# First modulation vector of a streaming-encoder layer: half of its weight rows go to TensorE, half stay on VectorE, and four token norms move behind the last VectorE sum

## The chip, the cores and the metric

The kernel runs on one core of one Trainium2 chip. A core has a matmul engine (TensorE, PE in the profile, with its weight loads shown as PEld), a vector engine (VectorE, DVE), an activation engine (ScalarE, ACT), a general engine (GpSimd, POOL) and a queue from which DMA transfers are issued (SyncE, SP). Each engine works through its own list of instructions in order and waits where an operand isn't there yet. The metric is the device time of one execution in microseconds (us); the median over runs is compared.

## The reference: what is computed

One layer of a transformer trunk over 1024 tokens of 1024 channels: a gated feed-forward block, a mixer with two kinds of attention, and a second feed-forward block. Ahead of each of the three, the tokens are normalised and modulated by a shift and a scale that come from one condition vector `c`:

```python
mod = (jax.nn.silu(c) @ w_ada[l] + b_ada[l]).reshape(b, N_SUB, 3, D_MODEL)
...
shift = mod[:, i, 0, None, :]
scale = mod[:, i, 1, None, :]
gate = mod[:, i, 2, None, :]
u = rms_norm(h, norm_pre[l, i]) * (1.0 + scale) + shift
return h + resid_w * gate * rms_norm(fn(u), norm_post[l, i])
```

The change touches the shift and scale of the first feed-forward block only (`i = 0`): a vector of 1024 values times a matrix of 1024 x 2048, in float32. Nothing of the first block's matmuls can use a channel before its shift and scale are known.

## The kernel before, in words

The matmuls of the feed-forward blocks work on float32 operands split into a high and a low part (`H` and `L`, type fp32r), three matmuls for each product. A 2x2 block scheme with seven products (Strassen's) is used for the three feed-forward matrices, so tokens come in two halves, channels in two halves.

The opening of the program is `start0_`. It loads the first 512 tokens (`xt[0..3]`, four tiles of 128 x 1024), normalises them on ScalarE, and then goes through four column blocks `cb` = 0 to 3. Block `cb` owns 256 channels of the shift and the same 256 of the scale, 512 columns in all. For each block:

- `matvec(cb)` loads the block's 1024 rows x 512 columns in four transfers of 512 KB (`w`, ring `row` of 8 buffers), two groups of 128 rows in each. Row group `k` is multiplied by the partition's own value of silu(c), `csil[:, k]`, and added up in `m` (128 x 512) on VectorE: one multiplication (L658) and seven multiply-adds (L660).
- TensorE sums `m` over its 128 partitions with a column of ones: four matmuls (L675) that write `mps`, 128 x 1 each. A float32 matmul shows as two instructions in the profile, so the profile counts 8 of L675 for a block. "The block's matvec products" below are these instructions.
- VectorE adds the bias and forms `bcol` and `acol`, the shift and scale as columns (L679 to L681).
- For the block's two channel groups `k`, TensorE transposes the four token tiles (L186), ScalarE applies scale and shift (`u`, L177), VectorE and GpSimd split it into `uH` (L179) and `uL` (L180).
- Feed-forward matmuls that need only the channels so far follow (L297 to L299, from `m.part`). Their weights come as `raw` tiles that ScalarE rounds to `wsH` and VectorE subtracts to `wsL` (L224, L225).

The sums of block `cb + 1` (`matvec(cb + 1)`) stand in the code ahead of block `cb`'s products. Tokens 512 to 1023 (`xt[4..7]`) are loaded during blocks 1 and 2 and normalised by `pre_norm` at the end of blocks 2 and 3: ScalarE squares and takes the root, VectorE inverts (L156) and scales the tile (L171). They are first used by the subtraction of the two token halves (L246) and by the transposes of `half1_blocks`, which feed the operands `T1`, `T2` and so on.

The order in which instructions stand on each engine is set by a scheduler that goes by its own estimates; `tc.keep_in_program_order` and `tc.issue_after` pin single instructions. SP issues a transfer only when the one eight places ahead of it has landed and the tile it fills is free.

Of the kernel before, what the change touches and what calls it, by code (L numbers as in the profile page):

```python
# [16 lines left out]
ALU = mybir.AluOpType  # L17
# [3 lines left out]
P = 128  # L21
D = 1024
S = 1024
NK = D // P
# [22 lines left out]
def build(ctx, tc, A, out):  # L47
    nc = tc.nc
    V, ACT, PE, POOL, SP = nc.vector, nc.scalar, nc.tensor, nc.gpsimd, nc.sync
# [10 lines left out]
    ones = const.tile([P, P], F32, name="ones")  # L60
# [4 lines left out]
    csil = const.tile([P, NK], F32, name="csil")  # L65
# [78 lines left out]
    def rstd_of(src, parts=1):  # L144

        junk = mpool.tile([P, D], BF16, name="junk", tag="junk", bufs=1)
        ss = mpool.tile([P, 2], F32, name="ss", tag="ss", bufs=4)
        w = D // parts
        for n in range(parts):
            ACT.activation(junk[:, n * w:(n + 1) * w], src[:, n * w:(n + 1) * w], AF.Square, scale=1.0 / 32.0, accum_out=ss[:, n:n + 1])  # L150
        if parts == 2:
            V.tensor_add(ss[:, 0:1], ss[:, 0:1], ss[:, 1:2])
        sq = mpool.tile([P, 1], F32, name="sq", tag="sq", bufs=4)
        ACT.activation(sq, ss[:, 0:1], AF.Sqrt, bias=eps)
        r = mpool.tile([P, 1], F32, name="rs", tag="rs", bufs=4)
        V.reciprocal(r, sq)  # L156
        return r
# [7 lines left out]
    def pre_norm(src, eng=V):  # L165

        r = rstd_of(src)
        if eng is ACT:
            ACT.mul(src, src, r)
        else:  # L170
            eng.tensor_scalar_mul(src, src, r)  # L171

    def modulate(mp, ps, k, half, ab, mtag="u32", bufs=3, eng=V):

        a, b = ab
        u32 = mp.tile([P, HALF], F32, name="u32", tag=mtag, bufs=bufs)
        ACT.activation(u32, ps, AF.Identity, bias=b[:, k:k + 1], scale=a[:, k:k + 1])  # L177
        H, L = u_tile("H", k, half), u_tile("L", k, half)
        V.tensor_copy(H, u32)  # L179
        eng.tensor_sub(L, u32, H.bitcast(F32))  # L180
        U[k, half] = (H, L)

    def transposed(psum, hn, k, half, tag):
        ps = psum.tile([P, HALF], F32, name="tps", tag=tag, **bank_bufs(tag))
        for q in range(4):
            PE.transpose(ps[:, q * P:(q + 1) * P], hn[4 * half + q][:, k * P:(k + 1) * P], ident)  # L186
        return ps
# [438 lines left out]
    xt = []  # L626

    def load_x(t):
        xt.append(y_tile(t))
        SP.dma_start(xt[t], A["x"][t * P:(t + 1) * P, :])  # L630

    def start0(fp, psum, mats):

        with tc.tile_pool(name="ff0", bufs=1, side="left", reuse_waits="tile") as sp:
            start0_(sp, fp, psum, mats)

    def start0_(sp, fp, psum, mats):
        raws = [sp.tile([P, 2, HALF], F32, name="raw0", tag="raw0", bufs=4) for _ in range(4)]
        for t in range(4):
            load_x(t)  # L640
        SP.dma_start(badaT, A["badaT"])
        SP.dma_start(npreT, A["npreT"])
        for t in range(4):
            pre_norm(xt[t], ACT)
        acol = const.tile([P, NK], F32, name="acol0")
        bcol = const.tile([P, NK], F32, name="bcol0")
        ab[0] = acol, bcol

        def matvec(cb):

            m = sp.tile([P, HALF], F32, name="m0", tag="m0", bufs=3)
            for kq in range(4):
                w = sp.tile([P, 2, HALF], F32, name="w0", tag="row", bufs=8)
                SP.dma_start(w, A["wada0"][cb, kq])
                for i in range(2):
                    cs = csil[:, 2 * kq + i:2 * kq + i + 1]
                    if kq == 0 and i == 0:
                        V.tensor_scalar_mul(m, w[:, i], cs)  # L658
                    else:
                        V.scalar_tensor_tensor(m, w[:, i], cs, m, ALU.mult, ALU.add)  # L660
            return m

        ms = [matvec(0)]
        for cb in range(4):
            ks = slice(2 * cb, 2 * cb + 2)
            if cb < 2:
                for i in (2 * cb, 2 * cb + 1):
                    mats[i].load(raws[i])
            for t in ((), (4, 5), (6, 7), ())[cb]:
                load_x(t)  # L670
            if cb < 3:
                ms.append(matvec(cb + 1))
            ps = psum.tile([P, HALF], F32, name="mps0", tag="y")
            for i in range(4):
                p = PE.matmul(ps[:, i:i + 1], ms[cb][:, i * P:(i + 1) * P], ones[:, 0:1], start=True, stop=True)  # L675
                if i == 0 and cb:

                    tc.keep_in_program_order(p)
            V.tensor_add(bcol[:, ks], ps[:, 0:2], badaT[:, ks])  # L679
            V.tensor_add(acol[:, ks], ps[:, 2:4], badaT[:, NK + 2 * cb:NK + 2 * cb + 2])  # L680
            V.scalar_tensor_tensor(acol[:, ks], acol[:, ks], 1.0, npreT[:, ks], ALU.add, ALU.mult)  # L681
            for k in (2 * cb, 2 * cb + 1):
                modulate(sp, transposed(psum, xt, k, 0, "y" if k % 2 == 0 else "pa"), k, 0, ab[0], mtag="u32", eng=V if cb == 3 else POOL)
            for t in ((), (), (4, 5), (6, 7))[cb]:
                pre_norm(xt[t])
            if cb < 2:
                for m in mats[:2]:
                    m.part()
            if cb == 1:
                for m in mats[2:4]:  # L690
                    m.part(2)
            if cb == 2:
                mats[0].part()
# [606 lines left out]
```

## Time and profile before

| | us |
|---|---|
| median of 3 runs | 2326.1 |
| lowest and highest run | 2325.53, 2331.6 |
| the profiled execution, its own time | 2332.79 |
| span of its trace, first to last instruction | 2331.0 |
| TensorE busy in the span | 2204.7 |
| VectorE busy in the span | 1570.6 |
| ScalarE busy in the span | 1047.5 |

Times in the trace count from the span's start. A busy TensorE isn't a TensorE at its peak: matmuls overlap each other, and the clock that is granted to the engine can be half of the full one. A row of the timeline gives start, duration, engine, line, operation, the tile written and the tiles read, how many instructions were merged, and in brackets how long the engine had been idle and what ended that.

### The profile page before, as it was taken

The page shows a single profiled execution, that of the slowest core. Times are in us where ns is not written, and L with a number is a line of the kernel's source. Part 1 is how long each engine was busy: PE and PEld are TensorE (multiplying, and loading weights), DVE is VectorE, ACT ScalarE, POOL GpSimd, SP SyncE. Part 2 cuts the span into 40 slices and gives each one's busy share as a digit, 9 for nine tenths or more (in the row PEclk, how much of TensorE's full clock was granted, in tenths as well). Part 3 has the DMA queues.
Part 4 walks back from the last instruction along what each step waited for, and adds up shares of the span by engine and source line. Part 5 has one row for each costly group of instructions (what it writes and reads, how often), then busy time and mean ns, then how long its engine had stood idle before and what let it go on. Part 6 is the DMA issues. An engine that isn't in the chain of part 4 may idle for free.

```text
span 2331.0 us, 28613 instructions
## 1 busy us (share of the span) xinstructions
PE 2204.7 (95%) x10420; PEld 1805.3 (77%) x10420; DVE 1570.6 (67%) x2612; ACT 1047.5 (45%) x1882; POOL 70.0 (3%) x90
## 2 busy tenths in 40 slices
PE   5989999989989989999999999999979999999998
PEld 3767788868868877878888888788767787877876
DVE  6885787566667587576677677665976666655565
ACT  4523333335445465454554455555723332325454
POOL 1000000000000010011001000000000000000000
PEclk8899999999999999999999999999989999999999
DMA  7283574358877211110111122764465443427667
GB/s 298 75 286 131 202 259 175 137 181 304 299 234 237 69 45 40 41 47 29 60 55 64 46 86 87 244 199 128 140 244 179 143 169 138 173 96 261 201 203 246
DMA packets 137678, 364.39 MB, mean 156 GB/s; under 512 B 16704, under 2 KB 20800, under 8 KB 137536
## 3 DMA queue, kind: packets, MB, share of 16 engines
q1 hardware_dynamic: 135904, 356.79, 45.0%
q0 software_dynamic: 1632, 5.77, 0.6%
q8 instruction: 81, 1.33, 0.2%
q14 instruction: 61, 0.50, 0.1%
HBM read 272.32 MB, written 90.18 MB: 156 GB/s over the span
## 4 chain that ended last, share of the span: by engine, by line
PE 67%; DVE 17%; DMA 8%; ACT 4%; issue 3%; SPq 0%; DVEq 0%; ACTq 0%
PE bank L299 9%; PE bank L297 9%; PE bank L298 9%; PE pps L765 4%; PE pps L763 4%; PE pps L767 4%; DMA stg<-in_wd 3%; DVE f L960 2%; PE bankA L547 2%; PE bankA L549 2%; PE bankA L548 2%; DMA stg<-d_T 2%; PE bankB L547 2%; PE bankB L548 2%; PE bankB L549 2%
## 5 line engine op out<-in xcount | busy, mean ns | idle before, releaser
L763 PE MATMUL pps<-uH,wsH 128*128 128x512 f32 x512 | 209.7, 410 | 0.0
L765 PE MATMUL pps<-uL,wsH 128*128 128x512 f32 x512 | 205.4, 401 | 0.0
L767 PE MATMUL pps<-uH,wsL 128*128 128x512 f32 x512 | 204.7, 400 | 0.0
L225 DVE TENSOR_TENSOR tbL<-stg,tbH 128x512 fp32r<-128x512 f32 x154 | 105.8, 689 | 113.7 <-ACT tbH L224 113.4
L224 ACT CAST tbH<-stg 128x512 fp32r<-128x512 f32 x154 | 95.6, 621 | 167.8 <-DMA stg<-d_T 98.6
L547 PE MATMUL bankA<-tbH,sbH 128*128 128x512 f32 x352 | 140.8, 402 | 18.3 <-ACT tbH L224 17.9
L297 PE MATMUL bank<-uH,wsH 128*128 128x512 f32 x352 | 141.4, 404 | 3.5 <-DVE uH L179 2.7
L298 PE MATMUL bank<-uL,wsH 128*128 128x512 f32 x352 | 140.3, 398 | 1.5 <-POOL uL L180 1.5
L548 PE MATMUL bankA<-tbL,sbH 128*128 128x512 f32 x352 | 140.4, 399 | 0.0
L549 PE MATMUL bankA<-tbH,sbL 128*128 128x512 f32 x352 | 139.6, 397 | 0.0
L299 PE MATMUL bank<-uH,wsL 128*128 128x512 f32 x352 | 139.2, 396 | 0.0
L224 ACT CAST wsH<-s 128x1024 fp32r<-128x1024 f32 x88 | 91.6, 1049 | 97.1 <-DVE s L331 88.0
L141 DVE TENSOR_TENSOR wsL<-raw,wsH 128x1024 fp32r<-128x1024 f32 x72 | 87.9, 1221 | 69.1 <-ACT wsH L140 67.5
L225 DVE TENSOR_TENSOR sbL<-stg,sbH 128x512 fp32r<-128x512 f32 (+1 forms) x176 | 108.8, 620 | 36.3 <-ACT sbH L224 34.6
L224 ACT CAST sbH<-stg 128x512 fp32r<-128x512 f32 (+1 forms) x176 | 98.9, 565 | 70.8 <-DMA stg<-hd_A 40.7
L364 ACT COPY q<-bank 128x512 f32<-128x512 f32 x44 | 25.8, 587 | 209.2 <-PE bank L299 209.2
L547 PE MATMUL bankB<-tbH,sbH 128*128 128x512 f32 x264 | 104.5, 396 | 11.3 <-ACT y L599 10.9
L767 PEld LDWEIGHTS pps<-uH,wsL 128*128 128x128 f32 x512 | 96.9, 189 | 17.9
L763 PEld LDWEIGHTS pps<-uH,wsH 128*128 128x128 f32 x512 | 97.6, 191 | 14.7
L225 DVE TENSOR_TENSOR wsL<-s,wsH 128x1024 fp32r<-128x1024 f32 x88 | 106.9, 1218 | 2.6 <-ACT wsH L224 2.0
L765 PEld LDWEIGHTS pps<-uL,wsH 128*128 128x128 f32 x512 | 97.2, 190 | 14.7
L548 PE MATMUL bankB<-tbL,sbH 128*128 128x512 f32 x264 | 104.2, 395 | 0.0
(247 smaller groups left out, 5947.7 us busy)
## 6 DMA issues: line engine op xcount, KB each, us to landing
wada<-in_wada SPq DMA_DIRECT2D x56, 512.0 KB, 5.6
raw<-in_wg SPq DMA_DIRECT2D x50, 512.0 KB, 6.7
raw<-in_wu SPq DMA_DIRECT2D x50, 512.0 KB, 4.4
raw<-in_wd SPq DMA_DIRECT2D x44, 512.0 KB, 4.5
stg<-hd_A SPq DMA_DIRECT2D x88, 256.0 KB, 4.3
stg<-d_S SPq DMA_DIRECT2D x88, 256.0 KB, 3.1
stg<-d_T SPq DMA_DIRECT2D x88, 256.0 KB, 3.5
d_S<-s SPq DMA_DIRECT2D x40, 512.0 KB, 2.7
```

The costliest lines, as they stand in the source:

```text
L141: eng.tensor_sub(l, raw, h.bitcast(F32))
L224: ACT.copy(h, src)
L225: V.tensor_sub(l, src, h.bitcast(F32))
L297: PE.matmul(ps, H[:, ks], bH, start=first and k == 0, stop=False, skip_group_check=not first)
L298: PE.matmul(ps, H[:, ks], bL, start=False, stop=False, skip_group_check=not first)
L299: PE.matmul(ps, L[:, ks], bH, start=False, stop=k == 3, skip_group_check=not first)
L547: PE.matmul(ps, sH[:, ts], tH, start=first, stop=False, skip_group_check=not check)
L548: PE.matmul(ps, sH[:, ts], tL, start=False, stop=False, skip_group_check=not check)
L549: PE.matmul(ps, sL[:, ts], tH, start=False, stop=last, skip_group_check=not check)
L763: PE.matmul(ps, aH, bH, start=i == 0, stop=False)
L765: PE.matmul(ps, aH, bL, start=False, stop=False)
L767: PE.matmul(ps, aL, bH, start=False, stop=i == n - 1)
```

## The change

Of the eight row groups of each column block, only groups 0 to 3 are still multiplied and added up on VectorE. Groups 4 to 7 go to TensorE straight from the loaded tile: for each of the four columns of `mps`, the tile's 128 x 128 piece is the stationary operand and `csil[:, k]` the moving one, accumulated on top of the sum of `m`. The norms of `xt[4..7]` leave blocks 2 and 3 and stand together in block 3, issued after the last multiply-add of block 3's `m`.

```diff
         def matvec(cb):
             m = sp.tile([P, HALF], F32, name="m0", tag="m0", bufs=3)
+            ws = []
             for kq in range(4):
                 w = sp.tile([P, 2, HALF], F32, name="w0", tag="row", bufs=8)
                 SP.dma_start(w, A["wada0"][cb, kq])
-                for i in range(2):
-                    cs = csil[:, 2 * kq + i:2 * kq + i + 1]
-                    if kq == 0 and i == 0:
-                        V.tensor_scalar_mul(m, w[:, i], cs)
-                    else:
-                        V.scalar_tensor_tensor(m, w[:, i], cs, m, ALU.mult, ALU.add)
-            return m
+                ws.append(w)
+            for k in range(4):
+                w, cs = ws[k // 2][:, k % 2], csil[:, k:k + 1]
+                if k == 0:
+                    V.tensor_scalar_mul(m, w, cs)
+                else:
+                    last_m[0] = V.scalar_tensor_tensor(m, w, cs, m, ALU.mult, ALU.add)
+            return m, ws
 
+        last_m = [None]
         ms = [matvec(0)]
...
             ps = psum.tile([P, HALF], F32, name="mps0", tag="y")
+            m, ws = ms[cb]
             for i in range(4):
-                p = PE.matmul(ps[:, i:i + 1], ms[cb][:, i * P:(i + 1) * P], ones[:, 0:1], start=True, stop=True)
+                cols = slice(i * P, (i + 1) * P)
+                p = PE.matmul(ps[:, i:i + 1], m[:, cols], ones[:, 0:1], start=True, stop=False)
                 if i == 0 and cb:
                     tc.keep_in_program_order(p)
+                for k in range(4, NK):
+                    PE.matmul(ps[:, i:i + 1], ws[k // 2][:, k % 2, cols], csil[:, k:k + 1], start=False, stop=k == NK - 1)
...
-            for t in ((), (), (4, 5), (6, 7))[cb]:
-                pre_norm(xt[t])
+            if cb == 3:
+                with tc.issue_after(last_m[0].ins):
+                    for t in range(4, 8):
+                        pre_norm(xt[t])
```

In the rows below L675 is the product with `m` before and L681 is the same one in the changed kernel; L686 is an added product with a loaded tile; L658 and L660 are L661 and L663, and L679 to L681 are L687 to L689.

TensorE at the last column block, from the first product with `m` on, before (`m_347`; the x4 are four float32 matmuls, eight instructions in the profile):

```order
L675 MATMUL mps_417<-ones,m_347 128x1 x4
L186 MATMUL tps<-ident,y_104 128x128
L186 MATMUL tps<-ident,y_106 128x128
L186 MATMUL tps<-ident,y_108 128x128
L186 MATMUL tps<-ident,y_110 128x128
```

and in the changed kernel (`m_367`; `w_372` and `w_374` are the block's third and fourth tile):

```order
L681 MATMUL mps_433<-ones,m_367 128x1
L686 MATMUL mps_433<-csil,w_372 128x1 x2
L686 MATMUL mps_433<-csil,w_374 128x1 x2
L681 MATMUL mps_433<-ones,m_367 128x1
L686 MATMUL mps_433<-csil,w_372 128x1 x2
L686 MATMUL mps_433<-csil,w_374 128x1 x2
L681 MATMUL mps_433<-ones,m_367 128x1
L686 MATMUL mps_433<-csil,w_372 128x1 x2
L686 MATMUL mps_433<-csil,w_374 128x1 x2
L681 MATMUL mps_433<-ones,m_367 128x1
L686 MATMUL mps_433<-csil,w_372 128x1 x2
L686 MATMUL mps_433<-csil,w_374 128x1 x2
```

Four matmuls have become twenty, and all of the added ones stand behind the first product with `m`, so none of them can run before VectorE's sum is done. The other three column blocks have the same rows.

ScalarE after the first norms, before (`raw_100` to `raw_103` are weight tiles, `u` the modulated channels):

```order
L224 CAST wsH<-raw_100 128x1024
L177 ACTIVATE u_205<-tps,bcol_147,acol_146 128x512
L224 CAST wsH<-raw_101 128x1024
L177 ACTIVATE u_216<-tps,bcol_147,acol_146 128x512
L224 CAST wsH<-raw_102 128x1024
L224 CAST wsH<-raw_103 128x1024
L177 ACTIVATE u_280<-tps,bcol_147,acol_146 128x512
L177 ACTIVATE u_291<-tps,bcol_147,acol_146 128x512
```

and in the changed kernel:

```order
L177 ACTIVATE u_213<-tps,bcol_147,acol_146 128x512
L224 CAST wsH<-raw_100 128x1024
L177 ACTIVATE u_224<-tps,bcol_147,acol_146 128x512
L224 CAST wsH<-raw_101 128x1024
L177 ACTIVATE u_300<-tps,bcol_147,acol_146 128x512
L224 CAST wsH<-raw_102 128x1024
L177 ACTIVATE u_311<-tps,bcol_147,acol_146 128x512
L224 CAST wsH<-raw_103 128x1024
```

Each rounding of a weight tile now stands behind a `u`, and so behind the shift and scale of its column block.

VectorE at the last column block in the changed kernel (`y_254`, `y_256`, `y_363`, `y_365` are `xt[4..7]`):

```order
L663 SCALAR_TENSOR_TENSOR m_367<-w_370,csil,m_367 128x512 x2
L156 RECIPROCAL rs<-sq 128x1 x3
L171 TENSOR_SCALAR y_254<-y_254,rs 128x1024
L171 TENSOR_SCALAR y_256<-y_256,rs 128x1024
L171 TENSOR_SCALAR y_363<-y_363,rs 128x1024
L687 TENSOR_TENSOR bcol_147<-mps_433,badaT 128x2
L688 TENSOR_TENSOR acol_146<-mps_433,badaT 128x2
L156 RECIPROCAL rs<-sq 128x1
L246 TENSOR_TENSOR y_104<-y_254,y_104 128x512
L689 SCALAR_TENSOR_TENSOR acol_146<-acol_146,npreT 128x2
```

Before, these scalings and subtractions stood between the multiply-adds of the last two blocks; now three scalings stand between the last sum and `bcol`, and one subtraction between the two steps of `acol`. The lists of all engines differ from those of before only in the opening, up to about the 400th TensorE instruction and the 180th of VectorE; from there on they have the same rows.

## The prediction

> **What bounds the kernel now.** The page comes first: where is TensorE not full?
>
> ```profile
> span 2331.0 us, 28613 instructions
> PE 2204.7 (95%) x10420; PEld 1805.3 (77%) x10420; DVE 1570.6 (67%) x2612; ACT 1047.5 (45%) x1882; POOL 70.0 (3%) x90
> PEclk8899999999999999999999999999989999999999
> ```
>
> TensorE is busy 95% of the span, and the two slices with a low granted clock are the first two, about 117 us. So the opening, where the change lies, is the weak place. Next, the opening in windows of 10 us (columns: length, then busy us and instructions of PE, PEld, DVE, ACT, POOL; granted clock, DMA share, GB/s):
>
> ```profile
> 10.00:20.00 10.00, 3.25 (x12) 2.10 (x11) 5.94 (x11) 6.48 (x10) 0.00 (x0) 1.00 1.02 405
> 20.00:30.00 10.00, 6.86 (x22) 4.25 (x22) 8.25 (x12) 4.27 (x5) 2.99 (x2) 1.00 1.03 421
> 40.00:50.00 10.00, 7.82 (x42) 6.46 (x40) 8.12 (x17) 4.92 (x10) 0.00 (x0) 0.99 0.52 199
> 50.00:60.00 10.00, 5.70 (x15) 2.92 (x15) 9.93 (x16) 2.31 (x4) 3.42 (x2) 0.52 0.02 5
> 60.00:70.00 10.00, 8.67 (x34) 7.25 (x34) 4.68 (x11) 3.01 (x5) 0.00 (x0) 0.50 0.17 52
> 80.00:90.00 10.00, 10.00 (x47) 8.23 (x47) 10.00 (x16) 6.18 (x11) 0.00 (x0) 1.00 0.43 133
> ```
>
> From 80 us on TensorE is full at full clock; whatever delays that point delays the end. Before it VectorE is the fuller engine in most windows, DMA saturates until the middle of the fourth window and then stops, and at 50 to 70 us TensorE has half its clock. The chain that ended last, cut to the first 90 us (start, us, what):
>
> ```profile
> by line: DVE m L660 17.4%; PE bank L297 10.8%; PE tps L186 10.4%; PE bank L298 8.7%; PE bank L299 8.6%; issue 7.1%; PE mps L675 6.6%; DMA y<-in_x 4.1%; ACT junk L150 3.7%; ACT y L169 3.5%; DVE y L171 2.5%; DVE wsL L225 2.1%; DVE uH L179 2.1
> ...
> 61.07 1.75 PE mps L675 x8
> 62.85 0.16 DVE bcol L679
> ...
> 63.22 1.10 PE tps L186 x4
> ...
> 64.39 0.79 ACT u L177
> ```
>
> The multiply-adds of L660 have 17% of these 90 us, some 15 us, and the products with `m` 6.6%. Each column block is one serial chain: sum on VectorE, products on TensorE, `bcol`, transposes, `u`. A saving on VectorE and a cost on TensorE therefore lie on the same path, one behind the other.
>
> **The prices.** The four blocks of products (starting 18.45 to 60.94), two starts at 390 us, where the same kind of product stands in a full TensorE, and VectorE's and ScalarE's rows:
>
> ```profile
> 18.45 1.87 PE L675 MATMUL mps<-ones,m 128*128 128x1 f32 x8 [2.14 <-DVE m L660]
> 32.69 1.30 PE L675 MATMUL mps<-ones,m 128*128 128x1 f32 x8 [3.36 <-DVE m L660]
> 48.68 1.02 PE L675 MATMUL mps<-ones,m 128*128 128x1 f32 x8 [1.88 <-DVE m L660]
> 60.94 1.87 PE L675 MATMUL mps<-ones,m 128*128 128x1 f32 x8
> ...
> 390.94 1.84 PE L101 MATMUL mps<-ones,macc 128*128 128x1 f32 x16
> 392.64 0.48 PE L297 MATMUL bank<-uH,wsH 128*128 128x512 f32 x1
> ```
>
> ```profile
> 14.51 3.88 DVE L660 SCALAR_TENSOR_TENSOR m<-w,csil,m 128x512 f32<-128x512 f32 x5
> 20.35 0.16 DVE L679 TENSOR_TENSOR bcol<-mps,badaT 128x2 f32<-128x2 f32 x1 [1.96 <-PE mps L675]
> 23.60 1.93 DVE L225 TENSOR_TENSOR wsL<-raw,wsH 128x1024 fp32r<-128x1024 f32 x1 [0.51 <-ACT wsH L224]
> 34.02 0.16 DVE L679 TENSOR_TENSOR bcol<-mps,badaT 128x2 f32<-128x2 f32 x1 [1.48 <-PE mps L675]
> 50.87 0.69 DVE L246 TENSOR_TENSOR y<-y,y 128x512 f32<-128x512 f32 x1
> 52.89 1.49 DVE L179 CAST uH<-u 128x512 fp32r<-128x512 f32 x1
> ```
>
> With an open clock a product takes 1.70 / 16 = 0.106 us (392.64 - 390.94). Closed it is about twice that, 1.87 / 8 = 0.23 with the tail of the last; I take 0.22. The second block, across a change of clock, gives 1.30 / 8 = 0.16. A multiply-add takes 3.88 / 5 = 0.78.
>
> **What the change removes:** 16 multiply-adds, 16 x 0.78 = 12.5 us of VectorE, about 3.1 a block. **What it adds:** 64 float32 matmuls, 128 instructions, 32 a block: 3.4 us a block open, 7.0 closed. All stand behind the sum on TensorE, so nothing hides them. Already at the open price a block gives 3.1 and takes 3.4.
>
> **Block by block.** At each block the clock of the same block before is taken, since a block starts after the same sort of wait.
>
> Block 0. Of the five multiply-adds that start at 14.51 one is left, so the sum is ready at 15.3 and not at 18.4. 40 closed products are 8.8 us, with one transpose among them 9.1: `bcol` at 24.4 in place of 20.35, +4.0.
>
> Block 1. Now the roundings of `raw_100` and `raw_101` stand behind `u` on ScalarE:
>
> ```profile
> 15.68 1.03 ACT L224 CAST wsH<-raw 128x1024 fp32r<-128x1024 f32 x1
> 21.85 0.78 ACT L177 ACTIVATE u<-tps,bcol,acol 128x512 f32<-128x512 f32 x1 [5.14 <-PE tps L186]
> ```
>
> The first used to run at 15.68, in ScalarE's idle time. From `bcol` to the next sum's end there are now a gap and four transposes (1.5), two `u` (1.4), two roundings (1.9), one `wsL` beside GpSimd (1.9), one multiplication and three multiply-adds (2.8): 9.5, so 33.9, and 34.5 with TensorE's twelve matmuls ahead. That eats the shorter sum. 40 products at 0.16 are 6.5: `bcol` at 41.0 in place of 34.02, +7.0.
>
> Block 2. Before, TensorE worked from `bcol` at 34.02 until its transposes ended, then waited 1.88 us for the sum:
>
> ```profile
> 45.76 1.03 PE L186 MATMUL tps<-ident,y 128*128 128x128 f32 x8
> ```
>
> These 12.8 us (46.8 - 34.0) of matmuls remain, while the sum, without norms and four multiply-adds, is ready after 9.5. So TensorE becomes the last: 41.0 + 12.8 = 53.8. This is where moving the norms pays, and it pays only the 1.88. 40 open products and five transposes are 5.0: 58.8 in place of 49.74, +9.0.
>
> Block 3. Gap and transposes 1.3, two `u` 1.4, a cast beside GpSimd 1.5, the sum 2.8: 65.8. 40 closed products: 74.6 in place of 62.85, +11.8. The three scalings queued behind the sum (0.75 each) run beside the products. What is queued behind them waits for nothing longer, except that one subtraction (0.69) stands inside `acol` and two more among the casts: +0.7, of which `uL` and then TensorE wait. Against it the matmuls that ran at half clock until 71 us may find it open: -0.7.
>
> **Transfers** cost nothing. The third and fourth tile of blocks 2 and 3 now wait for TensorE's last reader and not VectorE's; SP is stopped behind them.
>
> ```profile
> 18.07 4.06 SPq L654 DMA_DIRECT2D w<-in_wada  x4
> 26.95 5.94 SPq L654 DMA_DIRECT2D w<-in_wada  x4
> w<-in_wada SPq DMA_DIRECT2D x16, 512.0 KB, 8.7
> ```
>
> Block 2's last issue moves from 22 to 24.4 and block 3's from 32.6 to 41; with 8.7 us to landing they are there at 33 and 50, 20 and 15 us ahead of their products. The four weight transfers behind them have until about 76. If that cover were gone, every us that a tile came late would be one on the chain.
>
> **A second place.** Near 129 us TensorE waits 6 us for a rounding that follows L331:
>
> ```profile
> 125.96 1.28 DVE L91 SCALAR_TENSOR_TENSOR macc<-wada,csil,macc 128x1024 f32<-128x1024 f32 x1
> 127.16 0.68 DVE L331 TENSOR_TENSOR s<-s,raw 128x512 f32<-128x512 f32 x1
> ...
> 128.97 0.79 PE L297 MATMUL bank<-T2H,wsH 128*128 128x512 f32 x1 [6.13 <-ACT wsH L224]
> ```
>
> VectorE's list in the changed kernel has two L91 ahead of this L331 and not one: +1.2. Other rows there are swapped too; I bound that by 2 us either way.
>
> **Sum:** 11.8 + 0.7 - 0.7 + 1.2 = +13 us. The profiled execution took 2332.8 us, so 2346 for one like it. That execution lies 6.7 above the median of 2326.1, so the sum goes onto the median: **2339 us**.
>
> **The rivals.** *The clock opens on the added products.* They are an unbroken 4 to 9 us of work, and the trace has the clock open after such a stretch, at 71 us. Then the blocks 0, 1 and 3 cost about 6.9, 5.2 and 6.9 us, and the sum is 13 - 1.9 - 1.3 - 1.9 - 1 (matmuls behind them) = +7; if it also stays open between blocks (4.3 each after the first), +3: 2329 to 2333, not slower by what can be told. It decides where the mean price falls under 0.14 us. For it: nothing in the trace gainsays it. Against it: no stretch of these products alone is long enough to show it, and three transposes and products at 60 to 63 us, busy nearly all the time, left it at 0.50. [...]
>
> *They never open it, and close it.* [...] Then block 1 costs 8.8 and block 2 about 6.5 plus 2 for matmuls at half clock: 13 + 2.3 + 4 = +19, 2345. For it: 18.45 and 60.94 are closed.
>
> *Faster.* If TensorE could take the loaded tiles ahead of the sum, a block would end 3.1 us earlier and the chain shrink by up to 12 us, to 2314. It decides where an added product is done before the sum. Against it: in TensorE's list the product with `m` is first in every block. A small chance stays with VectorE's relief.
>
> **How the numbers follow.** Forecast (+9 to +15) 0.45, open clock (+2 to +8) 0.25, closed clock (+15 to +21) 0.2, faster 0.05, something at the second place or elsewhere 0.05. A measurement tells about 0.3% (7 us) from no change. Slower: the forecast, the closed case, some of the open one: 0.73; same 0.22; faster 0.05. The range leaves out the lowest and highest tenth: +2 to +21, 2328 to 2347.
>
> **What the new profile would show.** VectorE has 16 multiply-adds in L663, and VectorE's load at 40 to 60 us falls. Each block shows 40 products in one row, 4.2 to 8.8 us long, and `bcol` later than before, by about 4, 7, 9 and 12 us. ScalarE rounds `raw_100` after the first `u`. TensorE is full from about 90 us on. I am wrong if `bcol` of the last block comes before 66 us, if products take less than 0.1 us, or if the full stretch begins late and the end doesn't move.

## The result and the profile after

| | before | after |
|---|---|---|
| median | 2327.8 us (4 runs, 2325.5 to 2331.6) | 2345.9 us (4 runs, 2344.0 to 2347.2) |
| ratio to before, 95% interval | | 1.0068 [1.0051, 1.0086] |
| the profiled execution, its own time | 2332.8 us | 2346.9 us |
| span of its trace | 2331.0 us | 2345.1 us |

The changed kernel is slower by 18.1 us in the medians and by 14.1 us between the two profiled executions. (The ratio in the table isn't that of these two medians, 1.0078, which lies inside its interval.) One run of the kernel with 16 columns, at 3989.1 us, was in a slow state and is left out of that kernel's time below. The changed kernel's page (the span, the engines' busy time, and the granted clock in 40 slices):

```profile
span 2345.1 us, 28844 instructions
PE 2227.3 (95%) x10548; PEld 1828.6 (78%) x10548; DVE 1560.6 (67%) x2596; ACT 1048.3 (45%) x1882; POOL 70.6 (3%) x90
PEclk9799999999999999999999999999999999999999
```

TensorE has the 128 added instructions and 22.6 us more to do, VectorE 10.0 us less. The clock row reads higher in the first slice than before, but there it can't be compared: the trace holds no record of the clock ahead of 50.2 us (before: 26.5), and what has no record reads 1.00 (the last section comes back to this). The opening in windows of 10 us, with the columns as before:

```profile
30.00:40.00 10.00, 9.47 (x36) 7.86 (x35) 4.40 (x5) 0.00 (x0) 1.86 (x1) 1.00 0.76 263
60.00:70.00 10.00, 7.06 (x35) 4.72 (x35) 5.34 (x9) 4.11 (x8) 2.73 (x2) 0.69 0.17 52
70.00:80.00 10.00, 9.03 (x42) 9.00 (x43) 3.34 (x11) 0.00 (x0) 0.00 (x0) 0.50 0.01 2
80.00:90.00 10.00, 9.29 (x39) 7.53 (x38) 8.45 (x16) 5.63 (x8) 0.00 (x0) 0.61 0.18 53
90.00:100.00 10.00, 9.55 (x44) 7.34 (x43) 9.00 (x14) 9.72 (x16) 0.00 (x0) 1.00 0.27 82
```

VectorE, the fuller engine of the opening before, is busy for a third to a half of the windows shown up to 80 us; TensorE fills its windows from 90 us on and not from 80. VectorE's four `bcol` (the end of each column block's chain) in the timeline:

```profile
24.08 0.16 DVE L687 TENSOR_TENSOR bcol<-mps,badaT 128x2 f32<-128x2 f32 x1 [8.89 <-PE mps L686]
44.06 0.16 DVE L687 TENSOR_TENSOR bcol<-mps,badaT 128x2 f32<-128x2 f32 x1 [9.55 <-PE mps L686]
62.80 0.16 DVE L687 TENSOR_TENSOR bcol<-mps,badaT 128x2 f32<-128x2 f32 x1 [8.31 <-PE mps L686]
79.27 0.16 DVE L687 TENSOR_TENSOR bcol<-mps,badaT 128x2 f32<-128x2 f32 x1 [6.66 <-PE mps L686]
```

They come 3.7, 10.0, 13.1 and 16.4 us later than the four of before (20.35, 34.02, 49.74, 62.85). The brackets are the finding in short: ahead of each `bcol` VectorE has been idle for 6.7 to 9.6 us and waits for TensorE's added products. The first 95 us of the chain that ended last, by line, put it so (before, L660 of VectorE stood first with 17.4%):

```profile
by line: PE mps L686 24.9%; PE tps L186 7.1%; PE mps L681 6.3%; issue 5.5%; PE bank L298 4.7%; POOL uL L180 4.6%; PE bank L299 4.5%; DVE m L663 4.1%; ACT u L177 4.0%; DMA y<-in_x 3.8%; ACT junk L150 3.5%; ACT y L169 3.3%; DMA raw<-in_wu 3.2
```

The last entry is a weight transfer issued at 83.3 us. TensorE doesn't wait for it: from 83 us up to the second place below its timeline shows one wait, 0.45 us for a ScalarE row.

TensorE's timeline gives the price. In each of the four blocks, eight added products:

```profile
22.20 1.84 PE L686 MATMUL mps<-csil,w 128*128 128x1 f32 x8
42.18 1.84 PE L686 MATMUL mps<-csil,w 128*128 128x1 f32 x8
61.73 1.03 PE L686 MATMUL mps<-csil,w 128*128 128x1 f32 x8
77.39 1.85 PE L686 MATMUL mps<-csil,w 128*128 128x1 f32 x8
```

Blocks 0, 1 and 3 run at the closed price to their end, block 2 at the open one. Windows cut to the 40 products of block 1 and to those of block 2 (with some transposes):

```profile
35.50:44.00 8.50, 8.50 (x41) 8.44 (x40) 0.00 (x0) 0.00 (x0) 0.00 (x0) 1.00 0.28 80
57.80:62.80 5.00, 4.97 (x47) 4.88 (x45) 0.00 (x0) 0.45 (x1) 0.00 (x0) 1.00 0.00 0
```

In block 1 TensorE has 8.5 us of work without a gap, 0.21 us an instruction, and the clock doesn't open: the price is the closed one to the end, and the 1.00 in its row stands ahead of the first record.

The second place, where TensorE waits for a rounding that follows L331 (6.13 us ahead of 128.97 before), and VectorE's rows ahead of it:

```profile
143.75 1.27 DVE L91 SCALAR_TENSOR_TENSOR macc<-wada,csil,macc 128x1024 f32<-128x1024 f32 x1
145.55 1.27 DVE L91 SCALAR_TENSOR_TENSOR macc<-wada,csil,macc 128x1024 f32<-128x1024 f32 x1
146.75 0.68 DVE L331 TENSOR_TENSOR s<-s,raw 128x512 f32<-128x512 f32 x1
148.56 0.79 PE L297 MATMUL bank<-T2H,wsH 128*128 128x512 f32 x1 [8.71 <-ACT wsH L224]
```

The wait has grown by 2.6 us, and this matmul comes 19.6 us later than before. The two profiled executions end only 14.1 apart because of a wait far behind, in the second feed-forward block. Its row in TensorE's waits (us in total, times, the longest), before:

```profile
PE bankB L547 <- ACT y L599: 10.9, 2, 9.0
```

and after:

```profile
PE bankB L547 <- ACT y L599: 5.2, 1, 5.2
```

19.6 less these 5.7 is 13.9. In the other profiled executions below, this wait lies between 4.6 and 9.9 us, so it differs by a few us from one trace to the next. The medians (18.1) hold the chain's delay better than the pair of spans does.

### The profile page after: what moved, and what is told of

Its sections match the earlier page's. It is cut to its first block, busy times and chain, and to the rows that moved or that the text cites. A ratio compares the mean times of both kernels' runs of the same rounds, so it can differ in the third digit from the quotient of the medians.

```text
span 2345.1 us, 28844 instructions
## 1 busy us (share of the span) xinstructions
PE 2227.3 (95%) x10548; PEld 1828.6 (78%) x10548; DVE 1560.6 (67%) x2596; ACT 1048.3 (45%) x1882; POOL 70.6 (3%) x90
## 4 chain that ended last, share of the span: by engine, by line
PE 71%; DVE 16%; DMA 6%; ACT 4%; issue 2%; POOL 0%; SPq 0%; DVEq 0%; ACTq 0%
PE bank L299 10%; PE bank L297 9%; PE bank L298 9%; PE pps L775 4%; PE pps L773 4%; PE pps L777 4%; PE bankA L547 3%; PE bankA L548 3%; PE bankA L549 3%; DVE f L970 2%; PE bankB L547 2%; PE bankB L548 2%; PE bankB L549 2%; PE vps L773 1%; PE vps L777 1%
```

## The experiments

The start of the four `bcol` in each kernel's profiled execution, and its times; each ratio is to the runs of the kernel before on the same chip. On the chips of the experiments these have medians of 2329.2 to 2330.4, so the rows are better compared by their ratios than by their medians, and the `bcol` are those of one execution each.

| kernel | `bcol` 0 to 3, us | median, us | ratio, 95% interval |
|---|---|---|---|
| before | 20.4, 34.0, 49.7, 62.9 | 2327.8 | |
| changed kernel | 24.1, 44.1, 62.8, 79.3 | 2345.9 | 1.0068 [1.0051, 1.0086] |
| products only | 24.2, 41.1, 61.7, 80.8 | 2342.4 | 1.0059 [1.0046, 1.0072] |
| norms only | 20.5, 33.9, 47.1, 59.9 | 2327.1 | 0.9994 [0.9982, 1.0006] |
| sum last | 23.2, 43.1, 62.8, 78.3 | 2341.6 | 1.0059 [1.0045, 1.0072] |
| 128 columns | 23.2, 39.0, 54.1, 66.9 | 2331.3 | 1.0010 [1.0000, 1.0020] |
| roundings early | 24.1, 40.5, 56.9, 73.8 | 2342.0 | 1.0059 [1.0039, 1.0079] |
| 16 columns, roundings early | 24.1, 40.5, 56.9, 73.4 | 2341.1, one run | none |
| 64 columns, roundings early | 24.4, 39.7, 55.7, 72.2 | 2336.4 | 1.0030 [1.0016, 1.0045] |
| 128 columns, products ahead | 23.0, 35.3, 50.1, 62.0 | 2326.1 | 0.9988 [0.9976, 0.9999] |
| the same, two row groups on TensorE | 21.2, 32.6, 45.9, 58.7 | 2323.5 | 0.9965 [0.9952, 0.9979] |
| the same, none | 20.7, 33.5, 45.8, 57.9 | 2324.0 | 0.9972 [0.9960, 0.9985] |

**Products only.** The change, with the norms put back at the ends of blocks 2 and 3:

```diff
-            if cb == 3:
-                with tc.issue_after(last_m[0].ins):
-                    for t in range(4, 8):
-                        pre_norm(xt[t])
+            for t in ((), (), (4, 5), (6, 7))[cb]:
+                pre_norm(xt[t])
```

> The change with the four norms put back to the ends of blocks 2 and 3, products on TensorE as in the change. Theory (the added products at closed clock behind each sum cost the time; moving the norms is worth 1 to 3 us): blocks of 40 products in 8.5 to 9 us where the clock is closed, bcol of block 3 at 79 to 83 us, time 2345 to 2350 us, as slow as the change. Rival (the norms queued behind the last sum cost it): 2324 to 2330 us, bcol of block 3 at 63 to 66 us.

Its ratio, 1.0059, lies inside the interval of the change's, so the products make the loss and not the norms; the time lies under the 2345 to 2350 expected. Block 1's products in TensorE's timeline of this kernel, and the windows on both sides of a change in their pace:

```profile
38.22 1.03 PE L686 MATMUL mps<-csil,w 128*128 128x1 f32 x8
39.11 0.36 PE L681 MATMUL mps<-ones,m 128*128 128x1 f32 x2
39.34 1.75 PE L686 MATMUL mps<-csil,w 128*128 128x1 f32 x8
```

```profile
35.60:39.70 4.10, 4.10 (x37) 4.10 (x35) 0.00 (x0) 0.00 (x0) 0.00 (x0) 0.97 0.52 169
39.70:41.10 1.40, 1.38 (x7) 1.29 (x7) 0.00 (x0) 0.00 (x0) 0.00 (x0) 0.50 0.00 0
```

By the products' pace (0.12 us an instruction from 35.94 on) the clock was open from about 36.0, as the block began; at 39.5 it closed inside the block, with TensorE busy for all of the 4.10 us of the first window. Block 2, which began with the clock open, did the same at 59.9. So the clock not only stayed closed through blocks of these products (8.5 to 8.8 us each in blocks 0, 1 and 3 of the changed kernel), it closed while they ran.

**Norms only.** All eight row groups on VectorE, and the norms behind the last sum:

```diff
...
-            for t in ((), (), (4, 5), (6, 7))[cb]:
-                pre_norm(xt[t])
+            if cb == 3:
+                with tc.issue_after(last_m[0].ins):
+                    for t in range(4, 8):
+                        pre_norm(xt[t])
```

> All eight row groups summed on VectorE as before, only the norms moved behind the last sum. Theory: sums of blocks 2 and 3 end earlier by up to 1.9 and 2.9 us, one scaling (0.75) and one step more stand before acol; bcol of block 3 at 58 to 62 us, time 2322 to 2328 us. Rival (the norms' new place costs the time): 2336 us or more, with bcol of block 3 early and the work behind it late.

No difference that can be told. The chain gains 2.6 us at block 2 and 2.9 at block 3, and the second place takes it back:

```profile
128.58 0.79 PE L297 MATMUL bank<-T2H,wsH 128*128 128x512 f32 x1 [8.87 <-ACT wsH L224]
```

Its wait is 2.7 us longer than before, with the same two L91 ahead of L331 as in the changed kernel; with the products only it is 6.37 us and one L91. So the longer wait needs no added products. The norms' new place alone doesn't make it either: the six kernels below with 16 to 128 columns have the norms there too, one L91 that close ahead, and waits of 6.1 to 6.7 us. It goes with the order that VectorE's list got.

**Sum last.** The added products ahead of the four with `m`:

```diff
+            for k in range(4, NK):
+                for i in range(4):
+                    PE.matmul(ps[:, i:i + 1], ws[k // 2][:, k % 2, i * P:(i + 1) * P], csil[:, k:k + 1],
+                              start=k == 4 and i == 0, stop=False, skip_group_check=True)
             for i in range(4):
-                cols = slice(i * P, (i + 1) * P)
-                p = PE.matmul(ps[:, i:i + 1], m[:, cols], ones[:, 0:1], start=True, stop=False)
+                p = PE.matmul(ps[:, i:i + 1], m[:, i * P:(i + 1) * P], ones[:, 0:1], start=False, stop=True, skip_group_check=True)
...
-                for k in range(4, NK):
-                    PE.matmul(ps[:, i:i + 1], ws[k // 2][:, k % 2, cols], csil[:, k:k + 1], start=False, stop=k == NK - 1)
```

> As the change, but in each block the added products stand ahead of the product with the sum, so that they need not wait for VectorE. Theory (TensorE's own time is the price: in blocks 0 to 2 it reaches the products when the sum is ready or nearly so): bcol of blocks 0 to 2 less than 2 us earlier than in the change, block 3 some 2 to 4 us, time 2339 to 2344 us. Rival (the wait behind the sum is the price): bcol of block 3 at 63 to 66 us and 2324 to 2331 us.

`bcol` comes up to 0.9 us earlier, in block 3 too, where 2 to 4 were expected. When TensorE gets to the products, the sum is ready or nearly so; the price is the products' own time, not a wait for the sum.

**128 columns.** Each product with 128 equal moving columns, of which the first is read:

```diff
+        cw = sp.tile([P, 4, P], F32, name="cw")
+        for k in range(4):
+            V.tensor_scalar_mul(cw[:, k], ones, csil[:, k + 4:k + 5])
...
-                p = PE.matmul(ps[:, i:i + 1], m[:, cols], ones[:, 0:1], start=True, stop=False)
+                p = PE.matmul(ps[:, cols], m[:, cols], ones, start=True, stop=False)
...
-                    PE.matmul(ps[:, i:i + 1], ws[k // 2][:, k % 2, cols], csil[:, k:k + 1], start=False, stop=k == NK - 1)
+                    PE.matmul(ps[:, cols], ws[k // 2][:, k % 2, cols], cw[:, k - 4], start=False, stop=k == NK - 1)
```

> As the change, but every product of the blocks has 128 equal moving columns in place of one (the weight loads are the same; the first column of each result is used). Four small multiplications on VectorE make the wide operand before the first tile lands. [...]

128 times the moving data, and the kernel is 14.6 us faster than the changed one in the medians (some 13.5 by the ratios). TensorE's timeline in block 0:

```profile
18.36 1.92 PE L689 MATMUL mps<-cw,w 128*128 128x128 f32 x8
20.49 1.54 PE L689 MATMUL mps<-cw,w 128*128 128x128 f32 x8
22.09 1.06 PE L689 MATMUL mps<-cw,w 128*128 128x128 f32 x8
```

A product costs the same as with one column while the clock is closed (some 0.21 us) and while it is open (0.11); but by that pace it opens inside the block, at 21.5 us, 6.1 us after the block's start. The order of ScalarE and VectorE is another one too, however: the first two roundings stand ahead of block 0's `u` and the next two ahead of block 1's, much as before the change, and at the second place one L91 stands ahead of L331 and the wait is 6.13 us, 2.6 less than in the changed kernel. The roundings needed a control.

**Roundings early.** The changed kernel with its one-column products, and `u` held behind the roundings on ScalarE:

```diff
...
-        ACT.activation(u32, ps, AF.Identity, bias=b[:, k:k + 1], scale=a[:, k:k + 1])
+        iu = ACT.activation(u32, ps, AF.Identity, bias=b[:, k:k + 1], scale=a[:, k:k + 1])
+        if half == 0 and k < 4 and mtag == "u32" and ab is n_first[0]:
+            tc.keep_in_program_order(iu)
```

> The changed kernel with one thing put back: ScalarE's roundings of the first weight tiles (raw_100 to raw_103) stand ahead of u again, as before the change and as in the run with 128 moving columns; the products keep one moving column. It is the control for that run, which had both. If the clock is the reason why 128 columns were 14 us faster, the products here still run closed (0.21 us each in blocks 0, 1 and 3, 8.7 us a block); the earlier roundings shorten only the chain behind block 0, where TensorE is nearly the last anyway: bcol of blocks 1 and 3 at 42 and 77 us, 1 to 3 us ahead of the changed kernel, time 2342 to 2345. Rival, the order of ScalarE and VectorE made the gain and not the clock: bcol of block 3 at 67 to 70 us, time 2331 to 2335.

Both forecasts missed: `bcol` of block 3 comes at 73.8, between 67 to 70 and 77. Of the 12.4 us that the kernel with 128 columns gained there, 5.5 came with the early roundings. Of the other 6.9, the four blocks of products themselves make 6.4: from the first start to the end they take 8.8, 6.4, 5.1 and 8.7 us here, and 7.7, 5.4, 4.6 and 4.8 with 128 columns. Most of this, 3.9 us, is block 3's, and there it isn't shown that the columns opened the clock: with 128 columns it opened 0.4 us after the block's first product, behind feed-forward matmuls. The line numbers are four higher in this kernel (L685 and L690 for L681 and L686). Its block 1, which now starts with an open clock:

```profile
35.29 1.03 PE L690 MATMUL mps<-csil,w 128*128 128x1 f32 x8
36.19 0.38 PE L685 MATMUL mps<-ones,m 128*128 128x1 f32 x2
36.43 1.85 PE L690 MATMUL mps<-csil,w 128*128 128x1 f32 x8
```

```profile
35.00:45.00 10.00, 10.00 (x52) 9.44 (x53) 4.28 (x7) 2.71 (x6) 1.29 (x1) 0.66 0.51 182
```

The products start at 34.04 and the clock closes at 36.4, in a window in which TensorE has not one idle moment. That is free of any question of order. The time, 2342.0, has an interval that covers the changed kernel's ratio; the traces, not the times, carry this split. The execution that was profiled is the fastest of the five (2332.1), but its opening isn't special: the kernel with 16 columns, next, has nearly the same `bcol` in an execution of 2341.1.

**16 and 64 columns.** The last kernel with products of 16 columns, and of 64:

```diff
...
+                out = slice(i * 16, (i + 1) * 16)
...
+                    PE.matmul(ps[:, out], ws[k // 2][:, k % 2, cols], cw[:, k - 4, 0:16], start=False, stop=k == NK - 1)
```

> The changed kernel with 16 moving columns in each product (a tile of csil repeated, as with 128 columns) and the roundings early. It asks how much has to move for the clock to open. Theory: the clock goes by the share of the time in which columns move through the array; 16 columns are an eighth of 128, so the clock stays closed as with one column: blocks of 8.7 us, bcol of block 3 at 75 to 79 us, 2340 to 2345. Rival: only a single column is special, and 16 open the clock within a block as 128 did: blocks of 5 to 7.7 us, bcol of block 3 at 65 to 70 us, 2330 to 2334.

> As the run with 16 moving columns, but with 64. If the clock goes by the share of the time in which columns move, 64 are half of what opened it and may do: products at 0.106 us from 3 to 6 us after a block's start, bcol of block 3 at 65 to 70 us, 2329 to 2335. If 64 don't do, blocks of 8.7 us and bcol of block 3 at 75 to 79 us, 2340 to 2345. Beside the runs with 1 and 16 columns in nearly the same order of instructions it tells the clock from the order.

16 columns do as one does: `bcol` within 0.4 us of the last kernel in all blocks (in block 3 ahead of the 75 to 79 expected), and the clock closes inside block 1 again. 64 columns stand between. Blocks 0, 1 and 3 in TensorE's timeline:

```profile
22.48 1.92 PE L694 MATMUL mps<-cw,w 128*128 128x64 f32 x8
38.57 1.06 PE L694 MATMUL mps<-cw,w 128*128 128x64 f32 x8
70.28 1.92 PE L694 MATMUL mps<-cw,w 128*128 128x64 f32 x8
```

They don't open a closed clock in a whole block of 8.8 us (0 and 3), but in two blocks of some 5 us they don't close an open one either (1, where it opened 0.8 us after the first product, behind feed-forward matmuls, and 2). My forecast, that half the columns may open it, is wrong. In block 0 of the kernels with 128 columns the clock opened 6.1 us after the first product here, and in the kernels below with products ahead 5.8 us after it with four row groups on TensorE and 2.9 us with two; in blocks of 1, 16 or 64 columns it stayed closed over 8.5 us and more. What the clock goes by, the share of the time in which columns move or something else, no run shows. How far into a block it changes isn't set by the products alone: in the traces of before, the changed kernel, products only, norms only, sum last and 128 columns the recorded changes lie whole multiples of 3.41 us apart (before: 33.28, 40.11, 50.35 and 70.83 us, so 2, 3 and 6 times), and where they fall in a block differs from trace to trace: block 1's clock closed 0.6 us after its first product before the change, and 3.8 us after it with the products only.

**Products ahead.** 128 columns, and the products of block `cb + 1` written right behind the transposes of block `cb`, so that the feed-forward matmuls fill TensorE's next wait:

```diff
             for k in (2 * cb, 2 * cb + 1):
                 modulate(sp, transposed(psum, xt, k, 0, "y" if k % 2 == 0 else "pa"), k, 0, ab[0], mtag="u32", eng=V if cb == 3 else POOL)
+            if cb < 3:
+                pss.append(products(cb + 1))
```

> A version that could beat both: 128 moving columns, and the products of block cb+1 written right behind the transposes of block cb, so that TensorE has them ahead of most of that block's feed-forward matmuls (L297 to L299), which then fill the waits for the next shift and scale. Theory (TensorE's own time ahead of bcol is the price, and its waits behind bcol are the cover): bcol of blocks 1, 2 and 3 near 37, 51 and 61 us in place of 39.0, 54.1 and 66.9 with 128 columns alone, time 5 us below that run, 2326, which is 3 us below the kernel before and hardly told from it. Rival: the added products only move the feed-forward matmuls behind them, TensorE is full either way, and the time stays at 2331 although bcol comes earlier.

`bcol` at 35.3, 50.1 and 62.0 and 2326.1 us: as expected, 5.2 us below 128 columns alone, and just below the kernel before (0.9988 [0.9976, 0.9999]). But is it the split that pays? Two more kernels put row groups back on VectorE, six of eight and all eight (in the latter `cw` and its products are gone, and only the product with `m` is left):

```diff
-            for k in range(4):
+            for k in range(6):
                 w, cs = ws[k // 2][:, k % 2], csil[:, k:k + 1]
...
-                for k in range(4, NK):
+                for k in range(6, NK):
```

> The version with the products ahead and 128 moving columns, but with six row groups summed by VectorE and two multiplied by TensorE: 24 products a block in place of 40. Theory (each added product is TensorE's time on the chain, and the gain of that version is its order and its clock, not the split): 16 products less a block, 1.7 us of TensorE, against 1.6 us more of VectorE: bcol of block 3 at 57 to 62 us, time 2322 to 2327, no slower than with four groups. Rival (the relief of VectorE makes the gain): 2328 or more.

> The same with all eight row groups summed by VectorE as before the change, the products with the sum ahead and 128 columns wide, and the norms behind the last sum. It asks whether the split is worth anything at all. Theory: VectorE's sums of 6.2 us a block fit beside TensorE's matmuls once the products stand ahead of them, and TensorE is spared 13.6 us at the open price: bcol of blocks 0 to 3 near 20, 32, 45 and 55 us, time 2318 to 2326, level with or below the version with four groups (2326). Rival: without the split VectorE is the last again at each block (3.1 us a block), bcol of block 3 at 62 us or later and the time at 2328 to 2332, as before.

Both lie lower still, 2323.5 and 2324.0, though their intervals touch that of the kernel with four groups. So the split has no share in the gain: it is there without it. What the three kernels share is the place of the products in TensorE's list, their width, and the norms behind the last sum, which were worth nothing alone; with no group on TensorE the width doesn't open the clock either (the eight products take 2.1 us in blocks 0 and 3), which leaves the place. That is by elimination: the place alone, with one column and the norms where they were, wasn't run. With nothing on TensorE, VectorE's `bcol`:

```profile
33.47 0.16 DVE L693 TENSOR_TENSOR bcol<-mps,badaT 128x2 f32<-128x2 f32 x1 [0.18 <-PE mps L672]
45.82 0.16 DVE L693 TENSOR_TENSOR bcol<-mps,badaT 128x2 f32<-128x2 f32 x1 [1.31 <-PE mps L672]
57.92 0.16 DVE L693 TENSOR_TENSOR bcol<-mps,badaT 128x2 f32<-128x2 f32 x1 [0.71 <-PE mps L672]
```

VectorE, idle 6.7 to 9.6 us ahead of these in the changed kernel, waits 0.2 to 1.3, and the last block ends 4.9 us earlier than before the change. Of these, 2.9 came with the norms only too, and were lost again at the second place (8.87 us); here, with one L91, that wait is 6.73. How much of the gain is the place and how much this order therefore stays open.

## Why the prediction was right, and where its sizes were off

The sign and the cause were right: on this chain a sum and a product stand one behind the other, VectorE gives 3.1 us a block, and TensorE takes 5.0 or 8.7 for a block's products, which took 1.0 to 1.9 before. The time, 2345.9, lies inside the range of 2328 to 2347, near its upper end and 7 us above the forecast of 2339. From the median that the sum was put onto it is +19.8: outside the forecast's own band (+9 to +15, chance 0.45) and in that of the second rival, *They never open it, and close it* (+15 to +21, 2345, chance 0.2). So the range holds because it took that rival in. By its steps:

- **Block 0**, +4.0 at `bcol`: measured +3.7. The closed price (0.22) was 0.21.
- **Block 1**, +7.0: measured +10.0. This is the term that was mis-sized. The prediction took the mixed price of the same block before, 0.16; the products ran closed throughout, 8.5 us and not 6.5, and began at 35.49 and not at 34.5. The second rival had 8.8 here and was right for this block, and the blocks of one column in which the clock closed under a busy TensorE (at 39.5 with the products only, at 36.4 with the roundings early) bear out that it can close; that a block 2 of 6.5 and 2 more follows from it, no run shows: it took 5.0 here. With the norms in their old place block 1 ran mostly open, and its `bcol` came at 41.1, the 41.0 of the forecast: what decides is whether the clock is open when the block starts and how soon it closes. That may be in part chance. With the norms in their old place the clock opened 0.4 us into the block; in the changed kernel it stayed closed, though a change could have fallen 1.0 us into it, by an estimate that counts back from the first record there (50.17) in the 3.41 us found between recorded changes. How often it falls one way or the other wasn't tested.
- **Block 2**, start 12.8 us behind `bcol` and 5.0 us of products: measured 13.7 and 5.0. TensorE became the last there, as said.
- **Block 3**, 7.0 us to the sum and 8.8 of products: measured 7.6 (the sum's last multiply-add ends at 70.4) and 8.7.
- **The roundings behind `u`** were seen as part of the 9.5 us that "eats the shorter sum". With them put back, block 1 ends 3.6 us earlier, 1.5 by its start and the rest because the clock is open when it starts (its feed-forward matmuls go from 0.43 to 0.23 us apart at 33.0, 1.0 us ahead of the block), and block 3 5.5 us. I had expected 1 to 3 of that experiment: the two terms, the roundings and the clock, aren't independent.
- **Tail**, +0.7 and -0.7: `acol` did wait for the one L246, but the clock stayed at 0.61 between 80 and 90 us, so nothing came back.
- **Second place**, +1.2 by one more L91: the mechanism is shown, and the wait grew by 2.6. The kernel with the norms only has it as well, without the products.
- **Transfers** at no cost: in no block did a product wait for a tile, though block 3's last issue ended at 44.4 and not at 41.
- **The sum**, 13 us onto the median: the last `bcol` was 4.6 later than forecast, the clock's 0.7 didn't come, the second place took 1.4 more. 13 + 6.7 = 19.7, and the matmul behind the second place came 19.6 later. The medians differ by 18.1; the median of before, with a fourth run, stands 1.7 above the one that the sum was put onto.

The rival in which the clock opens on the added products fell in blocks 0, 1 and 3, where it was closed. The one in which products go ahead of the sum was priced at 2314; with that order (sum last) nothing came of it, since TensorE gets there too late. Ahead of the feed-forward matmuls, and with 128 columns, an order does pay, and without the added products it pays no less. One sentence of the last part was a slip: L663 has 12 multiply-adds, 16 is the number that went.

## What to carry to other kernels

When a serial chain passes from one engine to the next, moving work from the first to the second exchanges one price for another (here 3.1 us a block for 3.4 or 6.8), and what seems to pay is to put the chain's step ahead of work that nobody waits for. Price an added matmul at both clocks that the trace shows, and don't take the clock of the same place before the change: here an instruction costs 0.11 or 0.21 us with 1 to 128 moving columns, and in blocks of 1, 16 or 64 columns the clock stayed closed over 8.5 us and more. Follow the order that the scheduler makes of the change on every engine; here an exchange of roundings that the diff doesn't show went with 5.5 us at the last block of the trace.

## What the runs showed of the hardware that was not expected

- A float32 product took the same time with 1, 16, 64 and 128 moving columns, 0.21 us an instruction closed and 0.11 open, so widening it cost TensorE nothing here. What the clock did went with the columns in these runs: with 1 and 16 an open clock closed 2.4 to 3.8 us into a block in five blocks (two of products only, one of sum last, one each of roundings early and 16 columns; in others, of some 5 us, the block was over first), with 64 a closed clock stayed closed in two blocks of 8.8 us and an open one open in two of some 5 us, and with 128 it opened in block 0 of all three kernels that have added products of that width, 2.9 to 6.1 us after the first product. The order of the instructions differs between these kernels too.
- The granted clock of a window can mislead. In the changed kernel the windows of block 1 and block 2 both read 1.00, though the products of the first took 0.21 us each, twice those of the second. The column is wrong in the first: in the traces of before and after the first record of the clock is of an open one (from 50.17 us on in the changed kernel, from 26.46 before), and ahead of it the column reads 1.00, in the changed kernel's block 0 too, whose products took 0.21 us each. Feed-forward matmuls of one shape tell the same. They start 0.43 us apart ahead of block 1 and 0.23 us apart at 92 us, both in windows that read 1.00:

```profile
34.22 0.63 PE L298 MATMUL bank<-uL,wsH 128*128 128x512 f32 x1
34.65 0.63 PE L299 MATMUL bank<-uH,wsL 128*128 128x512 f32 x1
...
92.08 0.39 PE L298 MATMUL bank<-uL,wsH 128*128 128x512 f32 x1
92.31 0.40 PE L299 MATMUL bank<-uH,wsL 128*128 128x512 f32 x1
```

The durations are what to go by.
